# Modulation, value blocks and down phases re-placed in a two-layer diffusion block, with a larger DMA scratch

## The chip, the cores and the metric

The kernel runs on one core of one Trainium2 chip. Its time is the device time of one execution in microseconds (us). TensorE is called PE below, VectorE DVE, ScalarE ACT, GpSimd POOL and SyncE SP. The kernel before has a median of 1771.73 us over three runs (1768.1 to 1772.18).

## The reference

Two layers run over 512 latent tokens and 256 context tokens, 1024 wide, in fp32. Layer 0 mixes by gated linear attention and grouped attention, layer 1 by HGRN2 (a gated linear recurrence with eight heads). Each layer then has a SwiGLU feed-forward block (FFN). Each sub-layer is put between two RMS norms and is modulated by six vectors (shift, scale and gate, twice) that a matrix product of the conditioning vector gives:

```python
m_lat = jnp.split((sc @ mod_w[l] + mod_b[l])[:, None, :], 6, axis=-1)
h_lat = _modulate(_rms(x_lat, norm_pre_mix[l]), m_lat[0], m_lat[1])   # h * (1 + scale) + shift
...
x_lat = x_lat + m_lat[2] * _rms(o_lat @ w_out, norm_post_mix[l])
h_lat = _modulate(_rms(x_lat, norm_pre_ffn[l]), m_lat[3], m_lat[4])
x_lat = x_lat + m_lat[5] * _rms(_swiglu(h_lat, ffn_w_gate[l], ffn_w_up[l], ffn_w_down[l]), norm_post_ffn[l])
```

The context goes the same way with its own vectors `m_ctx`. Layer 1 needs the context only in its mixer, so its projection and FFN run over the 512 latent tokens alone.

## The kernel before, in words

**Products.** An fp32 product is made of three fp32r products (`mm3`): each operand is split into a high part H and a low part L (`wH`, `wL`; `aH`, `aL`), ACT making H and DVE making L. FFN products also use Strassen's scheme in Winograd's form. The gate and up products take seven block products instead of eight (`seven`, L799; PSUM tiles `a`, `b`, `E`, `D`). There are eleven blocks of columns; the first goes another way (`pearly`), the ten others take two `seven` each. The down product runs seven passes, "11", "S1", "N3", "SN", "S3", "22" and "12", over eleven row blocks in seven groups (`down`, L1605; PSUM tiles `x`, `o`, `q`). A down pass needs sums of weight blocks. These are built in the tiles `t` by DMAs which add what they load to what is there (`add`, L1629, `accum_op`). POOL issues them. There are 21 in each down phase, twelve of 512 KB and nine of 256 KB.

**Modulation.** Vector (l, m) of layer l needs eight loads of 512 KB from `mod_w` (tile `mraw`) by SP. `mod_vec` (L539) then multiplies and adds on DVE (`macc`, one instruction per load and stream), sums over the partitions on PE (`mod_acc<-macc`) and turns the result into columns (`modT`); a gate also goes through DRAM as a row (`gt`, `gd`). `mod_step` (L515) makes the products on PE instead (`mod_acc<-mraw`). Both are generators: code around them takes the next step at chosen places. A Tile scheduler then sets each engine's order of instructions from its own estimate of their times; stretches marked `pinned` keep the order of the code.

**Stages, with their times in the profile.** Start and first mixer to 343; output projection `out_proj` (L1470) to 410; first block of FFN 0 to 452; the ten other blocks to 769; down phase 0 to 943; value products and the first head's gates (`odd_value`, L1289; the PSUM tiles `nat`, then `ff` and `fq`) to 1065; the eight heads to 1340; output projection 1 and first block to 1416; FFN 1 to 1620; down phase 1 to the end at 1766.

**What stands where before.** `late_mods` (L1911) does (0,5) with `mod_step`, then (1,0) and (1,1) with `mod_vec`, in the first FFN: each `seven` calls `fill` twice (from the second of the ten blocks on), and each fill takes two steps. The values of the first half of the columns bring (1,2) and (1,3), `odd_mixer` (L1295) brings (1,4) and (1,5) beside the second half. Where the change and the prediction write (2,3), (4) or (4,5) of the value stage, layer 1 is meant. In `down` the operands of at most three groups are made ahead, from the phase's start on. A norm (`post_norm` L675, `pre_norm` L642) is issued in one piece: sum of squares, root on POOL (`rs`), scaling. The turn of the normed rows (`turns`) is put behind.

Of the kernel before, what the change touches and what calls it, by code (L numbers as in the profile page):

```python
# [17 lines left out]
P = 128  # L18
D = 1024
# [45 lines left out]
class Forms:  # L65
# [6 lines left out]
    def __init__(self, net, order, f, pool):  # L72
# [3 lines left out]
        self.place("11", pool.tile([P, 8 * self.n], F32R, name="b11"))  # L76
# [240 lines left out]
class Net:  # L317
# [3 lines left out]
    def __init__(self, ctx, tc, I, out):  # L321
# [5 lines left out]
        self.turns = []  # L327
# [187 lines left out]
    def mod_step(self, l, m, then=None):  # L515

        self.mod_tiles(l, (m,))
        acc = self.tr_tile("mod_acc")[:, :256]
        for k in range(KD):
            u = self.mod_loads(l, (m,), k, None, 2)[0]  # L520
            yield
            for j in range(4):
                self.mm(
                    acc[32 * j : 32 * j + 32, :],
                    self.scT[:, k, :],
                    u[:, 256 * j : 256 * j + 256],
                    start=(k == 0),
                    stop=(k == KD - 1),
                    tile_position=(0, 32 * j),
                )  # L530
        turned = self.mod_cols(l, acc, 256, [(m, r, 0, 0, r, 4) for r in range(2)])
        yield
        turned()
        if then:
            rows = self.gate_rows(l, *then)
            yield
            rows()

    def mod_vec(self, pool, jobs, own=None, bufs=2, sums=2):  # L539
# [7 lines left out]
        for l, ms, then in jobs:  # L547
# [19 lines left out]
            for j in range(4):  # L567
# [3 lines left out]
                    accs[j // 2][:, (j % 2) * 512 : (j % 2) * 512 + 512],  # L571
                    start=True,
# [69 lines left out]
    def pre_norm(self, pool, t, xt, A, B, h):  # L642
# [4 lines left out]
        rs = self.rstd(self.sumsq(xt, xn), D)  # L647
        nc.vector.tensor_scalar(xn, xt, rs, None, op0=ALU.mult)
# [19 lines left out]
        return turn  # L668
# [6 lines left out]
    def post_norm(self, y, x, gv, cuts=1, done=None):  # L675
# [5 lines left out]
        for i, c in enumerate(cs):  # L681
            self.sumsq(y[:, c], ss=ss[:, i : i + 1])
            nc.vector.tensor_tensor(tmp[:, c], y[:, c], gv[:, c], op=ALU.mult)
        if cuts > 1:
# [3 lines left out]
        rs = self.rstd(ss, D)  # L688
        for c in cs:
            nc.vector.scalar_tensor_tensor(x[:, c], tmp[:, c], rs, x[:, c], op0=ALU.mult, op1=ALU.add)  # L690
            if done is not None:
                done(c)

# [582 lines left out]

    def wide_units(self, c0, to=()):
        w = self.I["odd_w_in"][0]
        to = list(to)
        src = lambda k: w[k * P : (k + 2) * P, c0 : c0 + 512].rearrange("(k p) m -> p k m", p=P)  # L1280
        return [self.unit(src(k), 2, 512, to=to.pop(0) if to else None) for k in range(0, KD, 2)]
# [7 lines left out]
    def odd_value(self, fi, h, c0, t, us):  # L1289

# [4 lines left out]
    def odd_mixer(self, h, fi):  # L1295
        nc, I = self.nc, self.I
        w = I["odd_w_in"][0]
        with self.pool("hg") as gp:
# [6 lines left out]
            for _ in mods:  # L1305
                pass
# [733 lines left out]
```

## Time and profile before

| | |
|---|---|
| median of three runs | 1771.73 us (1768.1 to 1772.18) |
| profiled execution, its own time | 1768.36 us |
| its span | 1766.6 us |
| granted TensorE clock, mean | 0.982 |
| PE busy, share of the span | 95% |
| DVE busy | 73% |
| ACT busy | 53% |
| POOL busy | 7% |
| moved by DMA | 204.81 MB |

In the tables of the profile a line of a stage gives the stretch, its length, and for each engine the busy time with the number of instructions, then the granted clock of TensorE, the share of the 16 DMA engines that is in use, and GB/s. In a group of instructions stand the line of the code, engine, operation, output and inputs, shapes, number; then busy time, mean of one in ns, and the engine's idle time just before them with what ended it (`<-`). A timeline has start, duration, instruction, and in brackets the idle time before it with its end. The chain of waits is followed back from the last instruction.

### The profile page before, as it was taken

To read this page: it belongs to the slowest core of one execution; us is meant where nothing else is said; L and a number is where in the kernel's file an instruction comes from. 1 tells how busy PE (TensorE), PEld (TensorE's weight loads), DVE (VectorE), ACT (ScalarE), POOL (GpSimd) and SP (SyncE) were. 2 spreads that over 40 slices of the span, in tenths; PEclk is the share of its full clock that TensorE was granted. 3 is DMA by queue.
4 is the path that set the end of the run, shared out by engine and by line. 5 is a ranking of instruction groups with operands and counts; after the bars stand their busy time and mean duration, and the time that the engine had idled before them with its cause. 6 is when DMAs were issued, how large, how long until landed. Compare 5 with 4: busy or idle time off the path is not lost.

```text
span 1766.6 us, 32663 instructions
## 1 busy us (share of the span) xinstructions
PE 1669.6 (95%) x13401; PEld 1488.6 (84%) x13401; DVE 1298.4 (73%) x2121; ACT 928.9 (53%) x1615; POOL 122.6 (7%) x135
## 2 busy tenths in 40 slices
PE   6999999999999899999999879999999999999976
PEld 5899987889998799987877668889888899998854
DVE  5889678736769976676677577787865699897956
ACT  5745568737433344445458235666644755554633
POOL 1004010000000000002211000000000000000220
PEclk9999999999999999999999989999999999999988
DMA  9641031233244422247636671121124243434754
GB/s 315 199 132 38 3 92 65 72 120 120 72 144 147 138 76 75 70 152 155 96 113 217 212 238 38 49 61 49 50 84 131 96 141 114 117 96 129 176 93 152
DMA packets 184962, 204.81 MB, mean 116 GB/s; under 512 B 7366, under 2 KB 142060, under 8 KB 184812
## 3 DMA queue, kind: packets, MB, share of 16 engines
q1 hardware_dynamic: 173760, 181.82, 32.9%
q0 software_dynamic: 9120, 17.30, 6.1%
q10 hardware_dynamic: 1932, 3.59, 0.6%
q8 instruction: 105, 1.72, 0.4%
q14 instruction: 45, 0.37, 0.1%
HBM read 193.23 MB, written 9.46 MB: 115 GB/s over the span
## 4 chain that ended last, share of the span: by engine, by line
PE 69%; DVE 11%; DMA 8%; issue 5%; ACT 5%; POOL 2%; SPq 0%; DVEq 0%; POOLq 0%; ACTq 0%
PE a L355 10%; PE nat L355 8%; PE ff L355 7%; PE E L355 6%; PE x L355 5%; PE oproj L355 5%; DMA mraw<-in_mod_w_dram 5%; PE o L355 3%; PE b L355 3%; PE D L355 3%; PE pearly L355 2%; DVE macc L561 2%; PE fq L355 2%; PE gqk L355 2%; PE S L355 1%
## 5 line engine op out<-in xcount | busy, mean ns | idle before, releaser
L355 PE MATMUL nat<-wH,x 128*128 128x256 f32 (+2 forms) x992 | 231.0, 323 | 4.9 <-ACT x L672 2.6
L355 PEld LDWEIGHTS nat<-wH,x 128*128 128x128 f32 x992 | 166.4, 190 | 22.7 <-ACT x L672 3.6
L759 DVE TENSOR_TENSOR wL<-raw,wH 128x1024 fp32r<-128x1024 f32 x120 | 146.2, 1221 | 51.4 <-ACT wH L758 51.0
L758 ACT CAST wH<-raw 128x1024 fp32r<-128x1024 f32 x120 | 125.6, 1052 | 106.6 <-PE b L355 33.0
L355 PE MATMUL nat<-wL,x 128*128 128x256 f32 (+2 forms) x496 | 158.6, 320 | 3.1 <-DVE wL L704 3.1
L704 DVE TENSOR_TENSOR wL<-raw,wH 128x1024 fp32r<-128x1024 f32 (+1 forms) x84 | 100.0, 1199 | 39.3 <-ACT wH L703 38.5
L355 PE MATMUL ff<-x,wH 128*128 128x512 f32 (+1 forms) x512 | 128.6, 342 | 0.0
L703 ACT CAST wH<-raw 128x1024 fp32r<-128x1024 f32 (+1 forms) x84 | 86.1, 1037 | 74.7 <-PE ff L355 16.9
L561 DVE SCALAR_TENSOR_TENSOR macc<-mraw,scT,macc 128x1024 f32<-128x1024 f32 x84 | 105.3, 1280 | 26.5 <-DMA mraw<-in_mod_w_dram 26.3
L631 POOL TENSOR_TENSOR rs<-ms,neghalf 128x1 f32<-128x1 f32 (+2 forms) x62 | 61.2, 988 | 828.8 <-DVE ms L629 828.5
L355 PEld LDWEIGHTS nat<-wL,x 128*128 128x128 f32 x496 | 94.3, 190 | 12.3 <-DVE wL L704 4.8
L355 PE MATMUL oproj<-wH,x 128*128 128x512 f32 x320 | 101.8, 395 | 0.4 <-ACT x L1222 0.4
L355 PE MATMUL x<-wH,aL 128*128 128x512 f32 x220 | 89.4, 407 | 9.1 <-DVE aL L1662 9.1
L1629 POOL DMA_DIRECT2D t<-in_ffn_w_down_dram x42 | 45.4, 1179 | 741.0 <-DVE wL L1661 623.8
L355 PEld LDWEIGHTS ff<-x,wH 128*128 128x128 f32 x512 | 88.1, 191 | 10.3
L355 PE MATMUL x<-wH,aH 128*128 128x512 f32 x220 | 89.5, 407 | 7.1 <-ACT aH L1660 5.4
L910 ACT COPY qkh<-arr 128x512 f32<-128x512 f32 x112 | 70.1, 642 | 49.1 <-DVE arr L915 35.0
L355 PE MATMUL x<-wL,aH 128*128 128x512 f32 x220 | 89.0, 404 | 5.5 <-DVE wL L1661 5.5
L355 PE MATMUL ff<-x,wL 128*128 128x256 f32 (+1 forms) x256 | 86.7, 339 | 0.0
L783 DVE TENSOR_TENSOR raw<-raw 128x512 f32<-128x512 f32 x120 | 82.7, 689 | 2.6
L915 DVE TENSOR_TENSOR arr<-arr,f 128x512 f32<-128x512 f32 x112 | 74.3, 686 | 3.8 <-ACT qkh L910 2.5
L355 PE MATMUL E<-T,wH 128*128 128x384 f32 (+1 forms) x320 | 70.5, 309 | 1.6 <-ACT wH L758 1.6
(391 smaller groups left out, 4523.9 us busy)
## 6 DMA issues: line engine op xcount, KB each, us to landing
mraw<-in_mod_w_dram SPq DMA_DIRECT2D x80, 512.0 KB, 4.1
raw<-in_ffn_w_gate_dram SPq DMA_DIRECT2D x44, 512.0 KB, 3.9
raw<-in_ffn_w_up_dram SPq DMA_DIRECT2D x44, 512.0 KB, 3.8
raw<-in_odd_w_in_dram SPq DMA_DIRECT2D x40, 512.0 KB, 3.8
t<-in_ffn_w_down_dram POOLq DMA_DIRECT2D x24, 512.0 KB, 5.8
raw<-in_ffn_w_down_dram SPq DMA_DIRECT2D x22, 512.0 KB, 4.7
mraw<-in_mod_w_dram SPq DMA_DIRECT2D x32, 256.0 KB, 6.1
raw<-in_even_w_in_dram SPq DMA_DIRECT2D x16, 512.0 KB, 3.8
```

Source lines behind the costliest of these rows:

```text
L355: return self.pin(self.nc.tensor.matmul(*a, **k))
L561: nc.vector.scalar_tensor_tensor(a, u, w, a, op0=ALU.mult, op1=ALU.add)
L631: nc.gpsimd.tensor_tensor(rs, ms, self.neghalf.to_broadcast([P, w]), op=ALU.pow)
L703: nc.scalar.copy(H[:, :m], raw[:, :m])
L704: nc.vector.tensor_tensor(L[:, :m], raw[:, :m], H[:, :m].bitcast(F32), op=ALU.subtract)
L758: self.nc.scalar.copy(H, f)
L759: self.nc.vector.tensor_tensor(L, f, H.bitcast(F32), op=ALU.subtract)
L783: add = lambda o, x, y: nc.vector.tensor_tensor(o, x, y, op=ALU.add)
L910: nc.scalar.copy(qkv[:, :, :, half, :], dst)
L915: nc.vector.tensor_tensor(dst, dst, tb, op=ALU.mult)
L1629: add = lambda o, src: self.pin(nc.gpsimd.dma_start(out=o, in_=src, accum_op=ALU.add))
```

## The change

1. **Output projection 0.** Modulation (1,0) moves here, by a new generator `mod_late`, through the three buffers `raw` of the weights. One step is taken with each unit of the projection after the first four.
2. **First FFN.** (0,5) is done by `mod_late` on DVE instead of `mod_step` on PE; (1,1) follows, then (1,5), which comes from the odd mixer. A fill takes one step of two DVE instructions instead of two steps. `mod_late` loads one step ahead with two buffers.
3. **Value products.** Both halves of the columns are made by one loop, two pairs of tiles sharing their weights; (1,2) with (1,3), then (1,4), are spread over it with a third buffer (`go`). The odd mixer starts with its heads.
4. **Down phases.** The generator `down` makes the first two groups of operands in the last `seven`, in the memory of a Strassen form that is no longer used (`two`); a third ring comes with the phase. The closing work of the last block (`todo`) and the first sums `t` follow after the third group.
5. **Norms.** `post_norm` and `pre_norm` are generators; in pass "12" each product block takes one or two of their steps (`tick`). Passes "22" and "12" go through their last groups token tile by token tile. The gate of layer 1 is loaded before pass "22" ends, and the closing order of `qp` and `ending` moves with it.
6. **`dynamic_dma_scratch_size`** goes from 1024 to 2048: the memory for descriptors of DMAs that POOL issues.

DVE in the first FFN, before: rows of `mod_vec` for (1,0), between the closing of products (`zy`, `go`, `qa`) and sums of weights (`ws`, `raw`).

```order
L561 SCALAR_TENSOR_TENSOR macc_6389<-mraw_6391,scT,macc_6389 128x1024
L561 SCALAR_TENSOR_TENSOR macc_6390<-mraw_6391,scT,macc_6390 128x1024
L561 SCALAR_TENSOR_TENSOR macc_6389<-mraw_6395,scT,macc_6389 128x1024
L561 SCALAR_TENSOR_TENSOR macc_6390<-mraw_6395,scT,macc_6390 128x1024
L829 TENSOR_TENSOR zy<-zy,b 128x384
L783 TENSOR_TENSOR ws<-raw 128x512
L561 SCALAR_TENSOR_TENSOR macc_6389<-mraw_6481,scT,macc_6389 128x1024
L561 SCALAR_TENSOR_TENSOR macc_6390<-mraw_6481,scT,macc_6390 128x1024
L561 SCALAR_TENSOR_TENSOR macc_6389<-mraw_6485,scT,macc_6389 128x1024
L561 SCALAR_TENSOR_TENSOR macc_6390<-mraw_6485,scT,macc_6390 128x1024
```

The same engine in the first FFN of the changed kernel, rows of `mod_late` for (1,1).

```order
L596 SCALAR_TENSOR_TENSOR macc_6799<-mraw_6887,scT,macc_6799 128x1024
L869 TENSOR_TENSOR go<-go,b 128x384
L596 SCALAR_TENSOR_TENSOR macc_6800<-mraw_6887,scT,macc_6800 128x1024
L823 TENSOR_TENSOR ws<-raw 128x512
L596 SCALAR_TENSOR_TENSOR macc_6799<-mraw_6932,scT,macc_6799 128x1024
L823 TENSOR_TENSOR raw<-raw 128x512
L596 SCALAR_TENSOR_TENSOR macc_6800<-mraw_6932,scT,macc_6800 128x1024
L823 TENSOR_TENSOR raw<-raw 128x512
L799 TENSOR_TENSOR wL<-raw,wH 128x1024
```

Four modulation instructions stood in a row; now single ones stand between the work on weights and products.

PE at the passage from the values to the first head, before: the head's gate products `ff`, then the sums over partitions and the turn of modulation (4) and (5), then the head's transposes `kcT`.

```order
L355 MATMUL ff_10607<-x_9643,wH 128x256
L355 MATMUL ff_10607<-x_9642,wL 128x256
L355 MATMUL mod_acc<-macc_10209,one 32x512 x2
L355 MATMUL mod_acc<-macc_10210,one 32x512 x2
L358 MATMUL modT<-ident,modrows 128x128 x4
L358 MATMUL gcT_10377<-ident,gc_10375 8x128
L358 MATMUL kcT<-ident,kc 128x128 x4
```

The same passage in the changed kernel: the last value products `nat`, the sums of (4), and then the head's first `ff`.

```order
L355 MATMUL nat<-wL,x_9587 128x512
L355 MATMUL nat<-wH,x_9588 128x512
L355 MATMUL mod_acc<-macc_10222,one 32x512 x4
L358 MATMUL modT<-ident,modrows 128x128 x4
L355 MATMUL ff_10324<-x_9585,wH 128x256
L355 MATMUL ff_10324<-x_9586,wH 128x256
L355 MATMUL ff_10324<-x_9585,wL 128x256
```

The sums of the last modulation stood behind the gate products of the head and now stand ahead of them.

DVE at the start of down phase 0, before: the last products are closed (`qa`, `qb`), then the low parts `aL` of the first groups are made.

```order
L836 TENSOR_TENSOR qa<-qa,E 128x384
L838 TENSOR_TENSOR qa<-qa,a 128x384
L839 SCALAR_TENSOR_TENSOR qb<-a,qb 128x384
L1584 TENSOR_TENSOR qa<-qa,go 128x768
L1585 TENSOR_TENSOR qb<-qb,go 128x768
L1662 TENSOR_TENSOR aL<-qa,aH 128x384
L1529 TENSOR_TENSOR qb<-qb,qa 128x384
```

The same place in the changed kernel, where the low parts are the tile `two`.

```order
L1711 TENSOR_TENSOR wL<-raw,wH 128x512
L878 TENSOR_TENSOR go<-go,a 128x384
L879 SCALAR_TENSOR_TENSOR go<-a,go 128x384
L799 TENSOR_TENSOR dL<-ws,dH 128x512
L1712 TENSOR_TENSOR two<-qa,two 128x384
L1719 TENSOR_TENSOR qa<-qb,qa 128x384
L1712 TENSOR_TENSOR two<-qa,two 128x768
L1719 TENSOR_TENSOR qa<-zy,qa 128x2x384
L869 TENSOR_TENSOR qb<-qb,b 128x384
```

The low parts of the first two groups now stand before the last products are closed.

The diff, cut to its core:

```diff
+    def mod_late(self, pool, jobs, tag="mraw", bufs=2, spare=None, per=1):
...
+        deep = bufs + (spare is not None) - 1
...
+            for _ in range(deep):
+                load()
+            yield
+            done = 0
+            for i, (k, m) in enumerate(steps):
+                if len(us) < len(steps):
+                    load()
+                u, us[i] = us[i], None
+                for a, (mm, r) in zip(accs, ms):
...
+                        nc.vector.scalar_tensor_tensor(a, u, w, a, op0=ALU.mult, op1=ALU.add)
+                    done += 1
+                u = None
+                if done % per == 0:
+                    yield
+
+            acc = self.tr_tile("mod_acc")
...
     def odd_mixer(self, h, fi):
...
-            us = self.wide_units(3 * D + 512)
-            mods = self.mod_vec(gp, ((1, ((4, 0), (5, 0)), (5, R_NQF, 1)),))
-            for t in (4, 5, 0, 1, 2, 3):
-                self.odd_value(fi, h, 512, t, us)
-                for _ in range(4):
-                    next(mods, None)
-            for _ in mods:
-                pass
...
+    def later(self, steps):
+
+        self.steps.append([self.steps[-1][2] + 2 if self.steps else 0, steps, 0])
+        self.steps[-1][2] = self.steps[-1][0]
+
+    def tick(self, n=1):
+        for _ in range(n):
+            if self.steps:
+                s = min(self.steps, key=lambda s: s[0])
+                s[0] += 1
+                if next(s[1], self) is self:
+                    self.steps.remove(s)
...
-    def out_proj(self, wop, pp, w, cat, tiles, end):
+    def out_proj(self, wop, pp, w, cat, tiles, end, mods=iter(())):
...
+                        if hf or t0:
+                            next(mods, None)
...
     def ffn(self, l, xp, yp, fp, pp, rp, h, ending, extra=None):
...
-        fill = lambda: [next(extra, None) for _ in range(2)]
+        fill = lambda: next(extra, None)
...
+            if idx == np_ - 1:
+                down = self.down(l, fp, qp, rp, xp, quad, early, tiles, n, ending, lambda: todo())
+                last = [lambda: None, lambda: next(down)]
...
-    def down(self, l, dp, fp, qp, xp, quad, early, y, tiles, n, ending):
+    def down(self, l, fp, qp, rp, xp, quad, early, tiles, n, ending, finish):
...
-        ahead_of = [ring()]
...
+        two = rp.tile([P, 8 * n], F32R, tag="b11", bufs=1, name="two").rearrange("p (e x m n) -> p e x m n", e=2, x=2, m=2)
+        rings = [[two[:, e, x] for x in range(2)] for e in range(2)]
...
+        ahead(2)
+        self.pinned = pinned
+        dp, y = yield
+        self.pinned = True
+        rings.append([dp.tile([P, 2, n], F32R, name=f"a{x}") for x in "HL"])
+        ahead(3)
+        for f in owed:
+            f()
+        finish()
...
-            if p == 6 and l:
-                tail = ng - 3
+            if p > 4:
+                tail = ng - 3 if p == 6 else ng - 2
...
+                if p == 5 and g == ng - 2 and i == 0:
+                    qp.release()
+                    end, final, (follow, begin) = ending(dp)
...
+                if p == 6:
+                    self.tick(2 if g < 3 else 1)
+                    if begin and g == tail - 1 and i == nh - 1:
+                        self.turn_next()
+                        begin(0, 0)
...
-        def late_mods(pool):
-            yield from self.mod_step(0, 5, (5, R_NQF))
-            yield from self.mod_vec(pool, ((1, ((0, 0), (0, 1)), None), (1, ((1, 0), (1, 1)), None)))
+        mods = self.mod_late(fp, ((1, ((0, 0), (0, 1)), None),), tag="raw", bufs=3)
+        forms, pp, rp = project(0, order, yp, I["even_w_out"][0], cat, xin, mods)
...
+        late = self.mod_late(
+            fp, ((0, ((5, 0), (5, 1)), (5, R_NQF)), (1, ((1, 0), (1, 1)), None), (1, ((5, 0),), (5, R_NQF, 1))), per=2
+        )
...
+                mods = self.mod_late(fp, ((1, ((2, 0), (3, 0)), (2, R_NQM, 1)), (1, ((4, 0),), None)), spare=spare)
+                for c in range(2):
+                    pairs = [order[4:], order[:2]][c]
+                    for t in order:
+                        if t == pairs[1]:
+                            continue
+                        ts = pairs if t == pairs[0] else (t,)
...
+                        if c == 0 and len(ts) == 1:
+                            self.turn_next()
+                            self.tick(5)
+                        if len(ts) == 1 and (c or t == order[3]):
+                            for _ in range(4):
+                                next(mods, None)
...
-    nc = bacc.Bacc("TRN2", target_bir_lowering=False, num_devices=1, dynamic_dma_scratch_size=1024)
+    nc = bacc.Bacc("TRN2", target_bir_lowering=False, num_devices=1, dynamic_dma_scratch_size=2048)
```

More of the change, by code (lines that the diff above doesn't have):

```diff
@@ L513, in mod_group @@
         turned()
[L515 to L537, printed above, removed]
     def mod_vec(self, pool, jobs, own=None, bufs=2, sums=2):
@@ L1491, in out_proj @@
             for t, pt in zip(pair, pts):
-                end(pt, t)
+                for _ in end(pt, t):
+                    pass
     def ffn(self, l, xp, yp, fp, pp, rp, h, ending, extra=None):
@@ L1742, in down @@
                     else:
-                        end(y0, t0)
+                        self.later(end(y0, t0))
         self.pinned = pinned
-        return follow
+        yield follow
     def run(self):
```

181 lines of the change are left out of this document (122 added, 59 removed).

## The prediction, made before the changed kernel had run

> **What bounds the kernel now.** I read the page first (busy time, the chain), then a table by stage, then, stage by stage, what TensorE (PE) waits for. From the page: the span, the engines' busy time, and the chain.
>
> ```profile
> span 1766.6 us, 32663 instructions
> PE 1669.6 (95%) x13401; PEld 1488.6 (84%) x13401; DVE 1298.4 (73%) x2121; ACT 928.9 (53%) x1615; POOL 122.6 (7%) x135
> PE 69%; DVE 11%; DMA 8%; issue 5%; ACT 5%; POOL 2%; SPq 0%; DVEq 0%; POOLq 0%; ACTq 0%
> ```
>
> PE is the bound, but 31% of the chain is not PE. The change leaves nearly all matmuls, so it can only win the stretches where PE stands. The table by stage (columns named in its first line) tells where those are.
>
> ```profile
> core 0: us, PE busy (x) PEld busy (x) DVE busy (x) ACT busy (x) POOL busy (x), PEclk, DMA share, GB/s
> 343.00:410.00 67.00, 66.97 (x348) 54.52 (x346) 24.34 (x33) 28.82 (x60) 4.97 (x9) 1.00 0.39 134
> 452.00:530.00 78.00, 78.00 (x487) 74.05 (x486) 51.77 (x72) 32.67 (x46) 0.00 (x0) 1.00 0.40 122
> 530.00:621.00 91.00, 80.51 (x439) 74.18 (x438) 83.41 (x103) 30.86 (x45) 0.00 (x0) 0.98 0.46 139
> 621.00:770.00 149.00, 148.27 (x855) 147.84 (x853) 98.97 (x137) 64.89 (x94) 0.00 (x0) 1.00 0.26 74
> 860.00:915.00 55.00, 54.42 (x241) 44.72 (x239) 37.83 (x49) 28.56 (x40) 5.97 (x6) 1.00 0.44 103
> 915.00:943.00 28.00, 21.97 (x97) 16.74 (x95) 22.50 (x32) 21.48 (x45) 6.05 (x5) 0.94 0.63 191
> 960.00:1010.00 50.00, 44.27 (x196) 32.88 (x195) 29.89 (x34) 18.80 (x38) 1.13 (x2) 1.00 0.71 218
> 1620.00:1660.00 40.00, 37.54 (x159) 30.51 (x158) 37.64 (x57) 23.74 (x40) 6.01 (x6) 0.96 0.74 198
> 1660.00:1729.00 69.00, 57.01 (x223) 44.57 (x222) 41.49 (x62) 29.19 (x47) 16.66 (x16) 0.90 0.69 126
> 1729.00:1766.00 37.00, 22.58 (x85) 17.46 (x83) 24.45 (x35) 14.36 (x26) 3.37 (x4) 0.79 0.43 157
> ```
>
> The unstalled row 860–915 gives 54.42/241 = 0.226 us for a 512-column matmul. At that price PE needs 223 x 0.226 = 50.4 of the 69 us of 1660–1729 (lost 18.6), 35.9 of 40 in 1620–1660 (lost 4.1), 19.2 of the last 37, 21.9 of 28 in 915–943 (lost 6.1). Busy time alone hides part of this, since matmuls after a stall are slower (PEclk 0.79 to 0.96). In the first FFN (452–770) PE idles 0 + 10.5 + 0.7 = 11.2 us.
>
> **First FFN: one modulation step per fill.** Groups of PE in 452–770, then one of DVE in 530–621:
>
> ```profile
> L355 PE MATMUL D<-x,wH 128*128 128x384 f32 x160 | 40.8, 334 | 0.0
> L355 PE MATMUL a<-b,wL 128*128 128x384 f32 x80 | 27.7, 347 | 5.8 <-DVE wL L759 5.8
> ...
> L355 PE MATMUL mod_acc<-mraw,scT 128*32 128x256 f32 x64 | 4.5, 387 | 0.0
> L355 PE MATMUL mod_acc<-macc,one 128*32 128x512 f32 x16 | 4.2, 602 | 2.3 <-DVE macc L561 2.2
> ```
>
> ```profile
> L561 DVE SCALAR_TENSOR_TENSOR macc<-mraw,scT,macc 128x1024 f32<-128x1024 f32 x28 | 34.5, 1280 | 3.9 <-DMA mraw<-in_mod_w_dram 3.8
> ```
>
> Seven groups of 160 and seven of 80 are the products: 1680 matmuls at 148.27/855 = 0.1734 us are 291.3 us, 29.1 for each of ten blocks. PE is busy 78.0 + 80.5 + 148.3 = 306.8, so 15.5 go elsewhere: two `mod_acc<-macc` groups (3.9), transposes and neighbours (about 3.5), and the 64 narrow matmuls of `mod_step`, about 8. These go; a third `macc` group with its transposes costs 2.5 back. Net -5.5 (ends -2, if narrow matmuls cost only their busy 4.5, and -6).
>
> The stall: DVE's own load is 98.97/149 = 66%, 19.3 us a block. With four fills a block, two steps each of two 1.28 us instructions, modulation adds 20.5: 39.8 us in 29.1. Hence DVE at 92% and PE idle in 530–621. Now a fill brings two such instructions, at most 10.2 a block (29.5), and on the whole 40 instructions over 28 fills, 7.3 a block: 26.6 of 29.1, 91%. I keep 3 of the 11.2 us of stall: -8 (ends: none gained, all gained). Loads for (0,5), (1,1), (1,5) are 24 at one ahead; they cost PE nothing as long as a load lands within a fill's 7.3 us. Together -13.5.
>
> **Output projection: +2.5.** Modulation (1,0) adds 16 x 1.28 = 20.5 us to DVE, busy 24 of 67 there: covered, if its eight loads come. They stand on SP behind the projection's weights and share their three buffers, at a DMA share of 0.39. Its column sums and turn on PE are not covered: 2.5 (0 to 6, the upper end if PE waits for the last steps).
>
> **Start of the down phases.** The third product of each phase, in PE's timeline:
>
> ```profile
> 772.20 0.50 PE L355 MATMUL x<-wH,aL 128*128 128x512 f32 x1 [2.92 <-DVE aL L1662]
> ...
> 1623.28 0.50 PE L355 MATMUL x<-wH,aL 128*128 128x512 f32 x1 [2.46 <-DVE aL L1662]
> ```
>
> Both wait for `aL`, which DVE made after closing the last block. Two operand groups, three of a pass's eleven blocks, are now made before, and the closing work stands behind the third: -5 (0 to -5.4).
>
> **Second down phase: the accumulating DMAs.** The DMA view from 1620 on (queue with its share of 16 engines; issues with size and time to landing), then POOL's timeline:
>
> ```profile
> q0 software_dynamic: 4560, 8.65, 37.0%
> ...
> t<-in_ffn_w_down_dram POOLq DMA_DIRECT2D x12, 512.0 KB, 5.8
> ...
> t<-in_ffn_w_down_dram POOLq DMA_DIRECT2D x9, 256.0 KB, 6.3
> ```
>
> ```profile
> 1636.92 0.92 POOL L1629 DMA_DIRECT2D t<-in_ffn_w_down_dram  x1 [241.13 <-DVE wL L1661]
> ...
> 1678.58 1.21 POOL L1629 DMA_DIRECT2D t<-in_ffn_w_down_dram  x1 [4.99 <-issue]
> 1684.70 1.21 POOL L1629 DMA_DIRECT2D t<-in_ffn_w_down_dram  x1 [4.91 <-issue]
> 1690.86 2.15 POOL L1629 DMA_DIRECT2D t<-in_ffn_w_down_dram  x2 [4.96 <-issue]
> ...
> 1725.28 0.88 POOL L1629 DMA_DIRECT2D t<-in_ffn_w_down_dram  x1 [3.77 <-issue]
> ```
>
> POOL waits for no semaphore ("issue"), yet starts one 512 KB add every 6.1 us, about its landing time, while two of 256 KB go as a pair: room for 512 KB in flight, as a full descriptor ring would look. Their data takes 37.0% of 146 us, 54 us, while they are spread from 1637 to 1725 and a landing, over 92; PE has some 18.6 us to lose by it. The scratch doubled lets two fly, and the pace then falls toward 54/21 = 2.6 us an add. What is late next: their loads share engines already 0.69 busy, so I take -15 (0, if the pace has another cause, to -18.6). The Trainium skill, page "SBUF — State Buffer", section "SBUF: two separate sides", speaks against: GpSimd, it says, cannot write descriptors while DVE holds the shared port, so DVE would set the pace and a larger ring nothing; by that the term is 0. DVE at 60% there with gaps this even does not look like it, but no run shows the lock itself.
>
> In the first down phase a pass is half again as long and 860–915 runs unstalled: no gain from the ring there.
>
> **Norms in steps.** Two pieces of the chain:
>
> ```profile
> 1730.96 5.56 DMA gv<-gd
> ...
> 1744.97 10.50 PE x L355 x34
> ```
>
> In the last stage PE ends at 1755.5; of 26.5 us it needs 19.2, so 7.3 are lost, after DVE stood 5.6 us for the gate's load, with the last operands behind it. The load is now issued a pass earlier: -5 (0 to -7.3; the norms after 1755.5 stay). In the first down phase 6.1 are lost around the norms; in steps between products: -4 (+2 to -6.1, since steps also delay operands).
>
> **Values and first head: 0.** Two pieces of the chain, first and last load of (2,3), then PE:
>
> ```profile
> 959.19 4.45 DMA mraw<-in_mod_w_dram
> ...
> 1002.67 1.29 DVE macc L561
> ```
>
> ```profile
> 1054.74 1.92 PE L355 MATMUL mod_acc<-macc,one 128*32 128x512 f32 x4 [7.79 <-DVE macc L561]
> ...
> 1063.45 0.63 PE L358 MATMUL kcT<-ident,kc 128*128 128x128 f32 x2
> ```
>
> Sixteen steps take 44.8 us, 2.8 each; PE then stands from 1046.95 to 1063.45 but for the sums, some 12 to 16 us, with the head's first products already done. Now (4) follows alone with eight steps, but its buffers are held by the turn of (2,3), and the order puts its `mod_acc` before the head's first products. About 4 + 8 x 2.8 = 26 us after the sums of (2,3), with 1.5 value tiles of 24 x 0.226 = 5.4 us between: a stall of 16 to 18. The other side gets back some of the 5.7 us idle in 960–1010. Sum 0 (-8 to +10).
>
> **Sum** against the profiled execution, 1768.4 (span 1766.6; the runs' median 1771.7 is 0.2% above): +2.5 - 13.5 - 5 - 15 - 5 - 4 + 0 = -40, 1728; half of the median's distance added, 1730.
>
> **Rivals.**
> 1. DVE, not the ring, paces POOL's adds: each add starts when a DVE instruction ends, and the term of -15 falls away: 1745. For it: DVE is 0.60 busy there, and some adds stand behind DVE's operands. Against: the even 6.1 us and the pairs. It is the page's rule named above that would make this so.
> 2. The ring is the limit, but the shared 16 engines are the next: they are 0.69 busy already, two adds in flight then land later than 5.8 us each and hold up SP's loads. A third of the term is left, -5: 1740.
> 3. DVE still saturates in the first FFN: 91% leaves 2.5 us a block and the steps come in runs of 101%. Stalls stay at 11 or grow to 20: 1738 to 1747.
> 4. The value stage loses, by the order and the buffers above, 10 to 20: 1740 to 1750. For it: the same chain of loads bounds the stage before, too.
> 5. Slower: each of the 24 first-FFN loads blocks DVE as in the value stage (4.45 us above), now that one is ahead where there were two: 24 x 4 = 96 us of DVE against 18 of slack (9% of seven blocks), +78, about 1808. It decides from (18 + 40)/24 = 2.4 us a load on. Against: 28 instructions waited 3.8 us in all before.
> 6. The change only moves the places where PE waits, and little arrives: 1764 to 1772.
>
> **How the numbers follow.** Forecast 0.62 (1717 to 1743: the terms' half ranges, about 6, 3, 2, 4, 4, 3 and 9 in the order of the parts, added as squares, give 13), rival 1 0.05, rival 2 0.09, rival 3 0.08, rival 4 0.08, rival 5 0.05, rival 6 0.03. The low end has every term at its good end: -62, 1706 by the profiled execution; the high end has two of rivals 1 to 4 together, 1730 + 15 + 11 = 1756. About 0.3% is what this measurement tells from no change: faster 0.92, same 0.03, slower 0.05.
>
> **What would show it.** Right: adds in pairs of 512 KB, 3 us apart, the second down phase some 20 us shorter; PE idle under 5 us in the first FFN with DVE near 90%; no `mod_acc<-mraw` there; no wait for `aL` at the down starts; a `mod_acc` wait of 16 us just before the first head's products, and none of 8 us after them. Wrong: adds still 6 us apart; DVE waiting for `mraw` in the first FFN; a wait for `mod_acc` beyond 25 us.

## The result, and the profile after

The changed kernel takes 1719.47 us (median of four runs, 1718.21 to 1724.71); the kernel before 1771.95 beside it. The ratio is 0.9712 with a 95% interval of 0.9687 to 0.9738: 2.9% faster, 52 us. The forecast was 1730 with a range of 1706 to 1756. The page of the changed kernel, its span, busy times and chain:

```profile
span 1716.3 us, 32583 instructions
PE 1649.0 (96%) x13359; PEld 1479.8 (86%) x13359; DVE 1313.2 (77%) x2138; ACT 929.7 (54%) x1615; POOL 131.0 (8%) x135
PE 79%; DVE 8%; DMA 6%; ACT 4%; issue 2%; POOL 0%; SPq 0%; DVEq 0%; POOLq 0%; ACTq 0%
```

PE's share of the chain rose from 69% to 79%, and "issue" fell from 5% to 2%; most of that fall is POOL's pacing in the second down phase, where "issue" was 35.6% of the chain from 1620 on and is 5.1% from 1596 on. The table by stage of the changed kernel, cut where its own stages begin (columns as before):

```profile
341.00:418.00 77.00, 76.97 (x399) 62.11 (x398) 48.37 (x60) 37.80 (x76) 9.34 (x10) 1.00 0.55 182
418.00:457.00 39.00, 35.33 (x210) 34.95 (x209) 36.06 (x41) 21.75 (x38) 2.32 (x2) 1.00 0.41 128
457.00:754.00 297.00, 296.89 (x1720) 292.89 (x1719) 238.33 (x316) 127.08 (x184) 0.00 (x0) 1.00 0.37 112
754.00:921.00 167.00, 162.19 (x711) 132.45 (x710) 123.65 (x160) 90.24 (x138) 29.09 (x28) 0.99 0.58 143
921.00:1044.00 123.00, 103.09 (x486) 83.16 (x485) 64.85 (x81) 48.80 (x88) 3.57 (x6) 0.90 0.53 168
1596.00:1707.00 111.00, 107.89 (x465) 85.98 (x464) 96.40 (x143) 66.75 (x108) 29.54 (x24) 1.00 0.72 175
```

In the first FFN PE has no idle time left (296.89 of 297), and the second down phase runs at full clock (1.00). The first block of the FFN (418–457) now loses 3.7 us, and the value stage (921–1044) is the one with most left to lose, 20 of 123.

Stage lengths in the two profiled executions, from PE's timeline, each from the first matmul of a stage to the first of the next:

| stage | before | after | change | forecast |
|---|---|---|---|---|
| start and first mixer | 342.0 | 341.1 | -1.0 | 0 |
| output projection 0 | 75.3 | 76.6 | +1.4 | +2.5 |
| first block of FFN 0 | 34.9 | 38.9 | +4.0 | 0 |
| ten blocks of FFN 0 | 316.4 | 297.1 | -19.4 | -13.5 |
| down phase 0, with its start | 174.5 | 167.1 | -7.4 | -6.6 |
| values and the first head's start | 120.3 | 123.7 | +3.3 | 0 |
| eight heads | 274.7 | 272.3 | -2.3 | 0 |
| output projection 1, first block, FFN 1 | 282.0 | 279.5 | -2.5 | 0 |
| down phase 1, to its last product | 137.7 | 110.8 | -26.9 | -22.4 |
| after the last product | 8.8 | 9.2 | +0.4 | 0 |
| span | 1766.6 | 1716.3 | -50.3 | -40 |

(The forecast's -5 for both starts is split -2.6 and -2.4.)

Each length comes from one profiled execution. In the runs below that leave every engine's order in a stage as the changed kernel has it (with the large scratch, for the last phase), the first block of FFN 0 takes 38.7 to 41.7 us, down phase 0 164.9 to 167.2, the values 120.6 to 124.4 and down phase 1 110.6 to 112.3. A change inside such a spread shows nothing by itself.

### The profile page after: what moved, and what is told of

Read it like the earlier page. It is cut to its first block, busy times and chain, and to the rows that moved or that the text cites. A ratio compares the mean times of both kernels' runs of the same rounds, so it can differ in the third digit from the quotient of the medians.

```text
span 1716.3 us, 32583 instructions
## 1 busy us (share of the span) xinstructions
PE 1649.0 (96%) x13359; PEld 1479.8 (86%) x13359; DVE 1313.2 (77%) x2138; ACT 929.7 (54%) x1615; POOL 131.0 (8%) x135
## 4 chain that ended last, share of the span: by engine, by line
PE 79%; DVE 8%; DMA 6%; ACT 4%; issue 2%; POOL 0%; SPq 0%; DVEq 0%; POOLq 0%; ACTq 0%
PE a L355 11%; PE nat L355 10%; PE ff L355 8%; PE x L355 8%; PE E L355 7%; PE oproj L355 5%; PE o L355 4%; PE D L355 4%; PE b L355 4%; DMA mraw<-in_mod_w_dram 3%; PE fq L355 3%; PE gqk L355 2%; PE q L355 2%; PE S L355 1%; PE poh L355 1%
## 5 line engine op out<-in xcount | busy, mean ns | idle before, releaser
L667 POOL TENSOR_TENSOR rs<-ms,neghalf 128x1 f32<-128x1 f32 (+2 forms) x62 | 69.9, 1131 | 861.0 <-DVE ms L665 860.8
L355 PE MATMUL x<-wH,two 128*128 128x512 f32 x310 | 102.4, 397 | 5.2 <-DVE two L1712 3.3
L596 DVE SCALAR_TENSOR_TENSOR macc<-mraw,scT,macc 128x1024 f32<-128x1024 f32 x70 | 89.1, 1279 | 14.0 <-DMA mraw<-in_mod_w_dram 13.8
L355 PEld LDWEIGHTS x<-wH,two 128*128 128x128 f32 x310 | 58.0, 189 | 20.5 <-DVE two L1712 6.5
L355 PE MATMUL a<-T,wH 128*128 128x384 f32 (+1 forms) x320 | 70.7, 310 | 0.3 <-ACT qb L861 0.2
L355 PE MATMUL E<-x,wH 128*128 128x384 f32 (+1 forms) x320 | 70.7, 310 | 0.0
```

The lines of the kernel that those rows point to most:

```text
L355: return self.pin(self.nc.tensor.matmul(*a, **k))
L596: nc.vector.scalar_tensor_tensor(a, u, w, a, op0=ALU.mult, op1=ALU.add)
L667: nc.gpsimd.tensor_tensor(rs, ms, self.neghalf.to_broadcast([P, w]), op=ALU.pow)
```

## The experiments

The theory to be tested had four parts: the descriptor ring paced POOL's adds; an overfull DVE made PE stand in the first FFN; the norms in steps, the gate's early load and the early operands won the rest of the down phases; and the value stage won nothing since its last modulation comes late. Stage lengths below are taken as in the table above.

### The ring: undone, and alone

```diff
-    nc = bacc.Bacc("TRN2", target_bir_lowering=False, num_devices=1, dynamic_dma_scratch_size=2048)
+    nc = bacc.Bacc("TRN2", target_bir_lowering=False, num_devices=1, dynamic_dma_scratch_size=1024)
```

> The changed kernel with dynamic_dma_scratch_size back at 1024 and nothing else changed. Theory (the descriptor ring paces POOL's adds): the adds of the second down phase start about 6.1 us apart again and PE waits for them, so the stretch from the first to the last product of that phase goes from 110.8 us to 123 to 130, and the kernel to 1732 to 1739 from 1719. Rival (DVE, or the work made early, paced them): the stretch stays within 3 us of 110.8 and the kernel at 1719 to 1722. Neither expects the first down phase to move by more than 2 us.

The second experiment is the kernel before with 2048.

> The kernel before with dynamic_dma_scratch_size 2048 and nothing else changed. Theory: the ring alone gives 15 to 18.6 us, so the second down phase goes from 137.7 us (first to last product) to 119 to 123 and the kernel from 1771.9 to 1753 to 1757; adds start 2.6 to 4 us apart. Rival (the larger ring helps only where operands are made early and norms are in steps): under 6 us, 1766 or more.

In both, all engines keep their order of instructions; only the scratch differs. With the small scratch the changed kernel takes 1743.94 us (1743.47 to 1747.1; ratio to the kernel before 0.9834, interval 0.9814 to 0.9855) and its second down phase 136.7 us, both above what the theory expected. With the large scratch alone the kernel before takes 1754.18 us (0.9890, 0.9868 to 0.9913) and its second down phase 120.2 us. POOL's timeline of the changed kernel, and the DMA view's row of its 512 KB adds in that phase (the last number is the time to landing):

```profile
1611.56 0.92 POOL L1677 DMA_DIRECT2D t<-in_ffn_w_down_dram  x1 [236.98 <-DVE wL L1711]
1613.16 1.22 POOL L1677 DMA_DIRECT2D t<-in_ffn_w_down_dram  x1 [0.68 <-DVE wL L1711]
1614.87 1.20 POOL L1677 DMA_DIRECT2D t<-in_ffn_w_down_dram  x1 [0.49 <-DVE wL L1711]
1617.47 1.21 POOL L1677 DMA_DIRECT2D t<-in_ffn_w_down_dram  x1 [1.41 <-DVE two L1712]
...
1653.40 1.21 POOL L1677 DMA_DIRECT2D t<-in_ffn_w_down_dram  x1 [2.35 <-issue]
...
1659.78 0.86 POOL L1677 DMA_DIRECT2D t<-in_ffn_w_down_dram  x1 [0.44 <-issue]
```

```profile
t<-in_ffn_w_down_dram POOLq DMA_DIRECT2D x12, 512.0 KB, 9.1
```

With the small scratch, the same kernel's POOL and the row of the stretch in which it paces:

```profile
1658.32 1.21 POOL L1677 DMA_DIRECT2D t<-in_ffn_w_down_dram  x1 [4.97 <-issue]
1664.09 1.21 POOL L1677 DMA_DIRECT2D t<-in_ffn_w_down_dram  x1 [4.56 <-issue]
1670.34 2.15 POOL L1677 DMA_DIRECT2D t<-in_ffn_w_down_dram  x2 [5.05 <-issue]
```

```profile
1640.00:1700.00 60.00, 47.02 (x180) 37.13 (x179) 32.12 (x47) 24.31 (x37) 13.70 (x14) 0.86 0.66 114
```

The 512 KB adds go mostly 1.6 to 4 us apart with the large scratch and about 6 with the small one, with one and the same work on DVE. The scratch is the cause: shown from both sides. That it works as a ring with room for so much in flight is read from the landing times in the traces. With the small scratch at most 768 KB are in flight, and most adds start 0.3 us after an older one has landed (1663.75, then the start at 1664.09 above; 1670.01, then 1670.34). With the large one up to 1.75 MB are in flight, and ten of the 21 adds still start so (1653.09, then 1653.40). So the ring still paces POOL there, but PE no longer waits for it.

That also settles, for this stage, the rule of the Trainium skill, page "SBUF — State Buffer", section "SBUF: two separate sides", weighed in the prediction: with DVE's lock as the pace, the scratch would have changed nothing, and it changed 17.5 us alone and 25.9 undone. No run shows the lock itself.

The two numbers differ, and that tells the rest: the other edits of the second down phase are worth 137.7 - 136.7 = 1.0 us behind the small ring and 120.2 - 110.8 = 9.4 with the large one. Where these 9.4 lie, PE's waits show; first the kernel before with the large scratch (1619 to 1740), then the changed one (1596 to 1708):

```profile
PE x L355 <- DVE aL L1662: 4.3, 2, 2.5
PE x L355 <- DVE wL L1661: 3.2, 1, 3.2
PE x L355 <- DVE y L1688: 1.2, 1, 1.2
```

```profile
PE x L355 <- DVE wL L1711: 1.0, 2, 0.7
PE x L355 <- DVE y L1752: 1.0, 1, 1.0
PE x L355 <- DVE two L1712: 0.7, 1, 0.7
```

They are 8.7 us in all against 2.7: 6 of the 9.4. Of the first three, 2.5 are the start of the phase; 3.2 and the other 1.8 come at 1720 to 1726, where DVE works through two whole norms before it makes the last pass's operands. The clock adds most of the other part: PE is busy 112.0 us there and 107.9 in the changed kernel, with the same matmuls. The granted clock is halved for 3.4 us behind the first of these waits and for 6.8 from the later pair on, and in the changed kernel nowhere in the phase.

### The first FFN: one step a fill, and (0,5) on PE

```diff
-        fill = lambda: next(extra, None)
+        fill = lambda: [next(extra, None) for _ in range(2)]
```

> The changed kernel with two modulation steps at each fill of the first FFN instead of one, so four DVE instructions of 1.28 us at a fill, as before. Theory (DVE is overfull while modulation runs: 66% of its own load and 20.5 us in 29.1): PE stands again, and the FFN's blocks take 6 to 12 us more than 297.1, the kernel 1725 to 1731. Rival (the stalls came with the narrow matmuls of the old way, not with DVE): under 2 us more, 1719 to 1722.

The blocks take 303.5 us, 6.4 more, and the kernel 1725.35 (0.9731, 0.9714 to 0.9748). The theory holds in kind: two steps a fill let PE stand again, some 4 us in these blocks, at the lower end of what was expected. The row of the blocks in this run (to be held against 457–754 above):

```profile
459.80:763.10 303.30, 299.23 (x1720) 294.37 (x1719) 237.47 (x315) 127.24 (x183) 0.00 (x0) 0.99 0.36 108
```

The other experiment here makes (0,5) on PE again:

```diff
+        def late_mods():
+            yield from self.mod_step(0, 5, (5, R_NQF))
+            yield from self.mod_late(fp, ((1, ((1, 0), (1, 1)), None), (1, ((5, 0),), (5, R_NQF, 1))), per=2)
...
+        late = late_mods()
```

> The changed kernel with modulation (0,5) made on PE again (64 narrow matmuls, one step at a fill), the rest of the modulations as in the changed kernel. Theory (narrow matmuls cost PE about 8 us and their way saves one macc group of 2): the FFN's blocks take 5 to 7 us more than 297.1, while the 3.8 us that PE loses in the FFN's first block, where DVE instructions of (0,5) stand ahead of the operands, come back: 1719 to 1724 in all. Rival (they lie beside other work and cost only their busy 4.5 or less): the blocks take under 2.5 us more, 1714 to 1719 in all.

The blocks take 301.6 us, 4.5 more, between the two expectations; the first block 34.9, 4.0 less; the kernel 1717.6 (0.9686, 0.9668 to 0.9704). PE's groups from 452 to 754 in this run:

```profile
L355 PE MATMUL mod_acc<-mraw,scT 128*32 128x256 f32 x64 | 5.1, 391 | 0.0
L355 PE MATMUL mod_acc<-macc,one 128*32 128x512 f32 x16 | 2.1, 604 | 0.0
```

The 64 narrow matmuls cost 4.5 plus what one group of sums over partitions takes in their place (2.5 by the forecast): about 7 us, where 8 were put down. PE does not wait in these blocks in either kernel, so this is their plain price. But with (0,5) off DVE the first block's loss is gone too, so the move from PE to DVE won about nothing in all.

### The first block

Seven instructions of (0,5), two short ones and five of 1.28 us, were ordered into the first block. PE's wait and two of the five ahead of it on DVE, in the changed kernel:

```profile
440.16 0.45 PE L355 MATMUL pearly<-x,wH 128*128 128x384 f32 x1 [3.67 <-DVE x L98]
```

```profile
434.29 1.28 DVE L596 SCALAR_TENSOR_TENSOR macc<-mraw,scT,macc 128x1024 f32<-128x1024 f32 x1
...
435.95 1.28 DVE L596 SCALAR_TENSOR_TENSOR macc<-mraw,scT,macc 128x1024 f32<-128x1024 f32 x1
...
439.42 0.68 DVE L98 TENSOR_TENSOR x<-f,x 128x512 fp32r<-128x512 f32 x1
```

```diff
-        fill = lambda: next(extra, None)
+        floor = []
+
+        def fill():
+            with self.tc.issue_after(floor[-1].ins):
+                next(extra, None)
...
-                    nc.vector.tensor_tensor(x[2 * i + half], g[:, i, tok], pts[i][1], op=ALU.mult)
+                    floor.append(nc.vector.tensor_tensor(x[2 * i + half], g[:, i, tok], pts[i][1], op=ALU.mult))
```

> The changed kernel, but the DVE instructions of modulation in the first FFN are held behind the last product of its first block, so that none of (0,5) stands ahead of that block's operands. Theory (PE loses 3.7 us there because five of them came before the operands x): the first block takes 34.9 to 35.5 us instead of 38.9, the other blocks 297 to 299, the kernel 1715 to 1717. Rival (DVE is merely full there, and the work comes back as a stall in the blocks): blocks above 300, 1718 to 1722.

The first block takes 34.9 us, the others 297.2, the kernel 1713.61 (0.9665, 0.9640 to 0.9690). The table's row for the block:

```profile
418.00:453.00 35.00, 35.00 (x208) 34.85 (x207) 29.84 (x34) 22.09 (x38) 1.95 (x2) 1.00 0.32 101
```

The theory holds: DVE was not too full there, it had the wrong thing first. In the runs that keep the order of the changed kernel in this block, its length went from 38.7 to 41.7 us, so 4 to 7 us were lost to it. The wait itself is about 3.5 to 4.4 us in all of them; the two shortest, of which the profile above is one, are those in which the clock was not halved behind it (the last section tells why).

### The value stage

PE's largest wait in the value stage of the changed kernel:

```profile
PE mod_acc L355 <- DVE macc L596: 14.6, 1, 14.6
```

The experiment takes (1,4) out of it and steps it beside the heads:

```diff
-                mods = self.mod_late(fp, ((1, ((2, 0), (3, 0)), (2, R_NQM, 1)), (1, ((4, 0),), None)), spare=spare)
+                mods = self.mod_late(fp, ((1, ((2, 0), (3, 0)), (2, R_NQM, 1)),), spare=spare)
...
+            mods = self.mod_late(gp, ((1, ((4, 0),), None),))
...
                 go(new, new)
+                go(mods)
                 go(scan, scan)
+                go(mods)
```

> The changed kernel, but modulation (1,4) is taken out of the value stage and made beside the first five heads of the odd mixer (two of its steps a head). Theory (the value stage gains nothing because PE waits 14.6 us for the last steps of (1,4) ahead of the head's first products): this wait goes, and its 3 us of sums and turn with it, so the values and the head's start take 105 to 109 us instead of 123.7; the heads take 1 to 4 us more; the kernel 1703 to 1708. Rival (the wait is only the one that comes last: loads of the head's weights or DVE's splitting of them are as late): 118 us or more for the stage, 1716 to 1720 in all.

The stage takes 105.5 us, 18.2 less, the heads 274.6, 2.3 more, and the kernel 1701.63 (0.9604, 0.9574 to 0.9635). The row of the stage in this run (to be held against 921–1044 above) and of the heads:

```profile
921.00:1026.00 105.00, 99.47 (x474) 81.03 (x473) 62.33 (x77) 49.13 (x88) 3.56 (x6) 0.97 0.62 197
1026.00:1301.00 275.00, 274.30 (x3258) 240.74 (x3256) 209.32 (x451) 164.93 (x281) 10.47 (x8) 1.00 0.20 59
```

Nothing else was late: PE's other waits in the stage come to 5.3 us in the changed kernel and to 5.4 here. The eight loads cost the heads, where the DMA engines are 0.20 busy, only 2.3 us.

### Norms, gate, operands, order of groups

Norms in one piece:

```diff
     def later(self, steps):
-        self.steps.append([self.steps[-1][2] + 2 if self.steps else 0, steps, 0])
-        self.steps[-1][2] = self.steps[-1][0]
+        for _ in steps:
+            pass
```

> The changed kernel with each norm issued in one piece where it is first called, in both down phases, as before, instead of in steps between the products. Theory (steps gain about 4 us in the first down phase and little in the second, where the gate's load was the larger part): the first down phase 169 to 173 us instead of 167.1, the second 111 to 114 instead of 110.8, the kernel 1722 to 1729. Rival (the merged order of the last groups gains it, not the steps): both within 1 us, 1719 to 1720.

Down phase 0 takes 168.7 us (+1.6), the values behind it 127.1 (+3.4), down phase 1 113.3 (+2.5); the kernel 1728.9 (0.9754, 0.9729 to 0.9779), of which 2.7 us more are in the first block of the FFN, whose order is the same. By this profile steps are worth 7.5 us, in both phases and in the stage after the first. All three lengths lie outside the spread given above, by 1.5, 2.7 and 1.0 us.

The gate asked for by the first norm, not before:

```diff
-            gates()
             return end, final, (ep.release, None)
```

> The changed kernel with the gate of layer 1 loaded when the first norm asks for it instead of a pass part earlier. Theory (DVE stands for that load, 5.6 us before, with the last operands behind it): the second down phase 114 to 117 us instead of 110.8, the kernel 1722 to 1726. Rival (with the operands three groups ahead the load is covered): within 1.5 us.

1720.56 us (0.9702, 0.9676 to 0.9729), second down phase 110.8. This run decides nothing on the load: every engine keeps the order of the changed kernel, and the load went out 23.9 us ahead of the last product, where it goes out 23.8 ahead in the changed kernel. What the load cost is seen elsewhere. DVE's wait for it and PE's longest wait behind it in the kernel before, then DVE's wait in the changed kernel:

```profile
1736.62 1.23 DVE L683 TENSOR_TENSOR pn<-y,gv 128x1024 f32<-128x1024 f32 x1 [0.84 <-DMA gv<-gd]
1742.64 0.79 PE L355 MATMUL x<-wL,aH 128*128 128x512 f32 x1 [5.05 <-DVE wL L1661]
```

```profile
1688.71 0.69 DVE L2074 TENSOR_TENSOR pl<-y,gv 128x512 f32<-128x512 f32 x1 [2.72 <-DMA gv<-gd]
```

The 5.6 us are the time of the load itself, from its issue at 1730.96 to its landing. DVE is at other work in most of that time, and stands for the load 0.8 us in the kernel before, not at all with the large scratch alone, and 2.7 in the changed kernel. So the early load saved DVE no wait. What PE waited for in the kernel before is a low part `wL` that DVE makes behind the norms which it works on from 1736.6 to 1741.4. The ring comes in only by the time of issue: ACT issues this load and stood for the adds, and with the large scratch alone the load goes out at 1711.7.

No operands asked for in the last block:

```diff
-        ahead(2)
         self.pinned = pinned
         dp, y = yield
```

> The changed kernel with no operands made in the last block: all three first groups of each down phase follow at its start (the closing work of the block stays behind them). Theory (PE waited for the low parts of the first group, 2.9 and 2.5 us before): the first products stand 2 to 3.5 us later in each phase, so the two down phases take 169 to 171 us instead of 167.1 and 113 to 114.5 instead of 110.8; the kernel 1724 to 1727. Rival (moving the closing work behind them is what counts): under 1 us in each, 1719 to 1721.

1717.86 us (0.9687, 0.9665 to 0.9709), both phases within 0.7 us. This decides nothing either: PE, DVE, ACT and POOL have the very order of the changed kernel, so the scheduler puts these operands where they were, since their memory is free. So another run puts them into memory that comes free only with the last block:

```diff
-        two = rp.tile([P, 8 * n], F32R, tag="b11", bufs=1, name="two").rearrange("p (e x m n) -> p e x m n", e=2, x=2, m=2)
-        rings = [[two[:, e, x] for x in range(2)] for e in range(2)]
+        rings = []
...
-        rings.append([dp.tile([P, 2, n], F32R, name=f"a{x}") for x in "HL"])
+        for _ in range(3):
+            rings.append([dp.tile([P, 2, n], F32R, tag=f"a{x}", bufs=3, name=f"a{x}") for x in "HL"])
...
         tp.release()
+        rp.release()
         dp = self.open_pool(f"d{l}")
```

> The changed kernel with the operands of each down phase in memory that comes free only with the last block, as before, instead of the tile two. The run with late operands had changed nothing since the scheduler still put them early; here they can't be early, while the closing work stays behind them. Theory (early operands give the 2.9 and 2.5 us of the down starts): the first products of each phase wait 1.5 to 3 us again, so down phase 0 takes 168.5 to 171 us instead of 167.1 and down phase 1 112.5 to 115 instead of 110.8; the kernel 1722 to 1726. Rival (it is the closing work behind them that counts): under 1 us in each, 1718 to 1721.

1721.63 us (0.9718, 0.9699 to 0.9737). PE's first wait in each down phase:

```profile
759.20 0.50 PE L355 MATMUL x<-wH,aL 128*128 128x512 f32 x1 [1.25 <-DVE aL L1711]
...
1599.37 0.50 PE L355 MATMUL x<-wH,aL 128*128 128x512 f32 x1 [0.72 <-DVE aL L1711]
```

Of the waits of 2.9 and 2.5 us, 1.25 and 0.72 come back; the other 1.7 and 1.7 stay away although the operands are late, which leaves the closing work that now stands behind. Phase 1 takes 112.8 us (+2.0, of which 0.5 lie outside the spread), phase 0 166.9 (-0.2), and the kernel's time is not clear of the changed kernel's. The waits decide here, not the times: they lie between the two expectations.

The old order of the groups in the passes "22" and "12":

```diff
-            if p > 4:
                 tail = ng - 3 if p == 6 else ng - 2
+            if p == 6 and l:
                 order = [(g, i) for g, i in order if g < tail] + [(g, i) for i in range(nh) for g in range(tail, ng)]
```

> The changed kernel with the passes 22 and 12 in the order of the kernel before: the token tiles in turn within each group, save the last pass of layer 1, which keeps its last three groups tile by tile. Theory (the first down phase gains some 4 us by steps and order together, of which the run with whole norms gave back 1.6): first down phase and values together 1 to 4 us more than 290.8, the second down phase within 1 us of 110.8; the kernel 1720 to 1724. Rival (the order does nothing): all within 1 us.

1720.24 us (0.9692, 0.9662 to 0.9721); down phase 0 and values together 288.5 us against 290.8, down phase 1 110.8. The order gains nothing that these runs show: the two stages together take 286.2 to 290.8 us in the runs that keep it.

### Both gains together

> The changed kernel with both moves that gained: modulation (1,4) beside the odd heads, and the first FFN's modulation held behind its first block. Theory (they lie in different stages and add up, -17.8 and -5.9): 1695 to 1698. Rival (one takes the other's place): 1700 or more.

1695.90 us (1695.24 to 1697.02; ratio to the kernel before 0.9559, interval 0.9541 to 0.9578). The two edits add up: values 105.2 us, first block 34.9, blocks 297.0. It is faster than both kernels, 4.4% under the kernel before and 1.4% under the changed one by the medians.

## Why the prediction was right

- **Ring: right, as the largest term.** -15 was put down, with an end of -18.6; alone it measured -17.5. The rivals with DVE or with the 16 engines as the next limit fell: those are 0.72 busy in the phase, an add lands in 9.1 us where it took 5.8, and still PE waits only 2.7 us in the whole phase.
- **First FFN: right in kind, too small.** The stalls went wholly, where 3 us were kept; and the working left out that matmuls after a stall are slower. The stalls were 10.5 us and not 11.2: the last 0.7 are the start of the wait at the down phase, which the window to 770 takes in and the term for the starts counts again. The net of narrow matmuls and sums was 5.5 by the forecast and 4.5 by the run with (0,5) on PE. That leaves 14.9 of the 19.4 us for the stall, 10.5 of it idle time. By the run with two steps a fill, 6.4 of these come from the lower density alone; how the rest divides between the moved modulation (1,0) and the end of the mix of PE's and DVE's ways wasn't separated. DVE was 84% busy in the seven blocks with modulation (174.75 of 208) and not 91%; seven of the 40 instructions had been done in the first block. It waited 1.3 us for these loads in the ten blocks and 2.0 in the first, so the slower rival, with 2.4 us a load as its point, was far off.
- **Norms in steps: right in the sum, wrong in one cause.** "The load is now issued a pass earlier: -5" was the step that failed, and with it its reading, that DVE stood 5.6 us for the gate: the piece of the chain is the load's own time, DVE stood 0.8 us, and it stands 2.7 in the changed kernel. What was won in that phase beside the ring are the norms that stood ahead of the last operands, and the start; that the sum of the phase held all the same is luck in this term.
- **Down starts: right in size** (no wait is left where 2.9 and 2.5 us were), half understood: by the waits, the closing work behind the operands won as much as the early operands or more (1.7 of 2.9 and 1.7 of 2.5).
- **Values: the mechanism and its size were right, the sum not quite.** The stall ahead of the head's first products was put at 16 to 18 us and measured 14.6. The sum came out at +3.3, within -8 to +10; the stage varies by 3.8 us between runs of one order, so it isn't known how much less came back on the other side.
- **Output projection: +1.4 for +2.5.** The loads were covered.
- **Not foreseen: the first block, +4.0.** "DVE busy 24 of 67" was worked out for the projection alone; the order of the changed kernel shows (0,5) ahead of the first block's operands, and that was not costed.
- **Not foreseen: -4.8 us from the heads to FFN 1.** Of these, 2.3 at most come from the first `pearly` of layer 1: it has a wait of 3.4 at 1390.9 in the kernel before, where the changed kernel has one of 1.1 for an operand, and one of 0.9 for a turn not far ahead. With the large scratch alone the 3.4 are still there, and in every run of the changed kernel's code, with the small scratch too, they are gone, so they went with the code; which edit removed them was not tested.

## What to carry to other kernels

Price a stall at more than its idle time where the clock drops behind it, and look at what an engine did during a DMA on the chain before calling the DMA's time its wait. Test a queue's depth alone before the work that waits for it is rearranged: behind the small ring the rearrangement of the last phase was worth 1 us, with the large one 9. Filler work for an engine with room belongs where the engine is least pressed and nothing near waits for it, not next to its consumer; eight loads that cost 18 us ahead of a head cost 2 beside the heads. A scheduler moves filler and operands by their memory and readiness, not by their place in the code, so a change of place alone may test nothing: look at the order it gives.

## What the runs showed of the hardware beyond this

What a wait costs in clock depends on when it falls. After PE's wait of 2.46 us at the start of the second down phase, in the kernel before, the matmuls a little later are slow for 3.4 us:

```profile
1624.10 0.63 PE L355 MATMUL x<-wH,aL 128*128 128x512 f32 x1
1624.52 0.63 PE L355 MATMUL x<-wH,aH 128*128 128x512 f32 x1
...
1627.08 0.56 PE L355 MATMUL x<-wH,aH 128*128 128x512 f32 x1
1627.48 0.39 PE L355 MATMUL x<-wL,aH 128*128 128x512 f32 x1
1627.71 0.39 PE L355 MATMUL x<-wH,aL 128*128 128x512 f32 x1
```

Eight start 0.42 us apart, where 0.23 is usual: 8 x 0.2 = 1.6 us more. The wait of 3.67 us in the first block of the changed kernel is longer, and no slow matmuls follow it. The rows of the kernel before around the first wait, then of the changed kernel around the second (PE's busy time is the first number behind the length, the granted clock the third from the end):

```profile
1620.63:1624.04 3.41, 0.95 (x4) 0.67 (x4) 3.41 (x8) 0.44 (x1) 0.00 (x0) 1.00 0.85 233
1624.04:1627.45 3.41, 3.41 (x9) 2.64 (x8) 2.82 (x5) 1.56 (x2) 0.00 (x0) 0.50 0.98 357
```

```profile
434.98:438.39 3.41, 1.51 (x9) 1.19 (x7) 3.41 (x5) 0.70 (x2) 0.00 (x0) 1.00 0.51 141
438.39:441.80 3.41, 1.64 (x9) 1.64 (x10) 3.41 (x5) 2.48 (x4) 0.00 (x0) 1.00 0.08 28
441.80:445.21 3.41, 3.41 (x22) 3.41 (x21) 3.41 (x4) 2.20 (x2) 0.00 (x0) 1.00 0.00 0
```

In each of the 14 traces here, all changes of the granted clock within the span lie whole multiples of 3.41 us apart, and its values are 1.0 and 0.5 alone. These rows are cut on that grid. The first wait lies in one stretch of it (2.46 us idle), and the clock is halved from its end on; the second is shared by two (1.90 and 1.77 us idle), and the clock stays. Over all traces, the 78 stretches at full clock that were followed by half clock had PE idle for 1.54 us or more, and the others, over 6700, for 1.93 at most. So about half a stretch of idle time was the limit, and where a wait fell on the grid decided between 38.7 and 41.7 us for the first block.

The Trainium skill, page "TensorE: Matmul & The Clock Gate", section "Part 1: The HAM clock gate (the "warmup" mystery)", has the clock halve after an idle window of about 3.4 us and come back after a busy one of that length. The traces agree on the half and on the 3.41 us, but a window need not be idle throughout: 2.46 us of it, and 1.54 at the least, were enough.

With up to five adds in flight a 512 KB add takes 9.1 us to land where it took 5.8 with up to three, and yet the 21 adds of the phase, which were spread over 88 us from first to last issue (1637 to 1725), now take 48 (1612 to 1660), and 51 in the kernel before with the large scratch alone: the deeper ring trades latency for throughput, as long as nothing waits for one add alone.
